# Gate and up tiles of two feed-forward blocks as seven block products, on one Trainium2 core

## The chip, the core and the metric

One core of one Trainium2 chip runs the whole program. The metric is device time in microseconds. Five engines work side by side, each with an instruction queue of its own: TensorE (PE in the rows, its weight loads PEld), VectorE (DVE), ScalarE (ACT), GpSimd (POOL) and SyncE (SP), which issues the loads. Instructions wait for one another through semaphores. TensorE writes PSUM, eight banks of 128 partitions x 512 float32.

## The reference, cut to what matters

One layer of a streaming encoder works on 288 tokens: 256 of a prompt and 32 new frames of a running stream.

```
h = x + 1/2 * swiglu(rmsnorm(x, g_ffn1), w1_gate, w1_up, w1_down)
h = h + token_mix(rmsnorm(h, g_mix), ...)          # pooling branch and attention
h = h + 1/2 * swiglu(rmsnorm(h, g_ffn2), w2_gate, w2_up, w2_down)
y = rmsnorm(h, g_final)

swiglu(x, wg, wu, wd) = (silu(x @ wg) * (x @ wu)) @ wd
```

The model width is 2048 (16 tiles of 128), the hidden width of each feed-forward block 5632 (44 tiles of 128). All data are float32. The change lies in the two swiglu blocks.

## The kernel before, in words

Tokens lie along the free dimension: an activation is 16 tiles of [128, 288], and a weight block of 128x128 is the stationary operand. To keep float32 accuracy at the speed of the shorter float32r type, each operand is split into a hi part (a cast) and a lo part (the difference), and each product is three matmuls: hi x hi, hi x lo, lo x hi (`mac`, lines 156 to 160).

The program is a list of steps (`step`, line 82). A step that needs weights names a source; `run` (line 91) issues its load on SyncE five steps ahead, splits it two steps ahead (`split_into`, lines 191 to 193: the cast on ScalarE, the subtraction raw - hi on VectorE; raw and hi lie both in SBUF), and then emits the step's matmuls. Work that follows a step, such as taking a result out of PSUM, is put off by `later`. So the order in each engine's queue is the order in which `run` emits.

`ffn` (line 279) takes the 44 hidden tiles in four chunks of 11. For each hidden tile it makes gate and up (16 blocks each, two loads of 128x1024), scales by the row norm, applies SiLU and the product, and splits the result (`post_g`, `post_u`). Then come 16 down tiles, each over the 11 hidden tiles of the chunk, added into h by `post_d` on VectorE. In the first block the first two hidden tiles are done apart, while the tokens arrive (`first_tiles`).

Between the two blocks lies the token mixer. Only one piece of it matters below: `post_z` (line 392) builds window sums on GpSimd (line 405), beside VectorE's subtractions of weights (line 193), and `scores4` and `attend4` (lines 707 to 734) use four column tiles of 32 for the new frames of four heads.

Of the kernel before, what the change touches and what calls it, by code (L numbers as in the profile page):

```python
# [33 lines left out]
CHUNKS = ((0, 11), (11, 22), (22, 33), (33, 44))  # L34
TB = T // 3

T_BUFS = 78
RAW_BUFS = 5
SPLIT_BUFS = 4
LOAD_AHEAD = 5  # L40
# [6 lines left out]
def kernel(ctx: ExitStack, tc: tile.TileContext, i, o):  # L47
# [10 lines left out]
    b4 = ctx.enter_context(tc.tile_pool(name="b4", bufs=4))  # L58
    psa = ctx.enter_context(tc.tile_pool(name="psa", bufs=8, space=bass.MemoryType.PSUM))
# [27 lines left out]

    def later(lag, fn):
        due.append((now[0] + lag, fn))

    def run():
        weighted = [k for k, s in enumerate(steps) if s[0] is not None]
        raws, splits = {}, {}
        at = [0, 0, 0]

        def load_to(n):
            while at[0] < min(n, len(weighted)):
                k = weighted[at[0]]
                src, m, _, extra, _, _ = steps[k]
# [3 lines left out]
                sp.dma_start(out=raw[:, :m], in_=src)  # L103
                raws[k] = raw
                at[0] += 1

        def split_some(n, count):

            while at[1] < min(n, len(weighted)) and count:
                k = weighted[at[1]]  # L110
                m, extra = steps[k][1], steps[k][4]
                if k not in splits:
# [13 lines left out]
                if c.stop == m:  # L126
                    raws.pop(k)
                    at[1] += 1

        done = 0  # L130
        load_to(LOAD_AHEAD)
        start()
        for k, (src, n, fn, _, _, late) in enumerate(steps):
            now[0] = k
            load_to(done + 1 + LOAD_AHEAD)
            split_some(done + 1, 99)
            if late is None:
                split_some(done + 1 + SPLIT_AHEAD, 99)
# [77 lines left out]
    def norm_part(st, x, first, last):  # L216
        if first:
            st["sum"] = acc()
        for j in range(3):
            pe.matmul(st["sum"][:TB, j : j + 1], x[:, j * TB : (j + 1) * TB], ones[:, 0:1],  # L220
                      start=first and j == 0, stop=last and j == 2)

    def norm_sum(st, width):
# [4 lines left out]
        v = sm.tile([TB, 3], F32, tag="v", name="v")  # L228
        dve.tensor_scalar(v, ps[:TB, 0:3], 1.0 / width, EPS, op0=ALU.mult, op1=ALU.add)
        r = sm.tile([TB, 3], F32, tag="r3", name="r3")  # L230
        pool.tensor_tensor(out=r, in0=v, in1=mhalf, op=ALU.pow)
        st["r3"] = r

    def norm_spread(st, scale=1.0, copy=True):
        ps = acc()
        for j in range(3):
            pe.matmul(ps[:, j * TB : (j + 1) * TB], st["r3"][:, j : j + 1].to_broadcast([TB, P]), ident[:TB, :TB],
                      start=True, stop=True)
# [12 lines left out]
    mhalf = cst.tile([TB, 3], F32, name="mhalf")  # L251
    prompt_p = [[cst.tile([P, (b + 1) * P], F32, name=f"p{q}{b}") for b in range(2)] for q in range(2)]
    gains = {n: cst.tile([P, w], F32, name=n) for n, w in
             (("g1", KD), ("gm", KD), ("g2", KD), ("gf", KD), ("gq", KL), ("gkv", KL), ("psc", 8))}
    cosT = cst.tile([P, T], F32, name="cosT")
    sinT = cst.tile([P, T], F32, name="sinT")
    inv16 = cst.tile([P, 4, 16], F32, name="inv16")
    hist = cst.tile([P, 8, HIST], F32, name="hist")

    krz = [cst.tile([P, S], F32, name=f"krz{j}") for j in range(2)]  # L260
    krh = cst.tile([P, SEQ], F32R, name="krh")
    krl = [cst.tile([P, SEQ], F32R, name=f"krl{j}") for j in range(2)]
    ckvh = cst.tile([P, KL, S], F32R, name="ckvh")
    ckvl = cst.tile([P, KL, S], F32R, name="ckvl")
    ckvn = cst.tile([P, KL, P], F32R, name="ckvn")
    pfar = cst.tile([P, P], F32, name="pfar")
    pnew = cst.tile([P, P], F32, name="pnew")
    osam = cst.tile([P, P], F32, name="osam")
# [9 lines left out]

    def ffn(wg, wu, wd, xs, st, last, together=None):
        extra = [lambda: norm_sum(st, D), lambda: norm_spread(st)]  # L280
        for c, (f0, f1) in enumerate(CHUNKS):
            mid = ({}, {})
            sv = {}

            def post_g(ps, m, sv=sv):
                z = col("z")
                dve.tensor_tensor(out=z, in0=ps[:, :T], in1=st["r"], op=ALU.mult)  # L287
                sv[m] = col("s")
                act.activation(sv[m], z, AF.Silu)  # L289

            def post_u(ps, m, sv=sv, mid=mid):
                u = col("u")
                dve.tensor_tensor(out=u, in0=ps[:, :T], in1=st["r"], op=ALU.mult)  # L293
                g = col("g")
                dve.tensor_tensor(out=g, in0=u, in1=sv.pop(m), op=ALU.mult)
                mid[0][m], mid[1][m] = split_dve(g, "m")

            if together is not None and c == 0:
                f0 += 2
                together(post_g, post_u)  # L300
            for m in range(f0, f1):
                for w, post in ((wg, post_g), (wu, post_u)):
# [3 lines left out]
                    if first:  # L306
                        step(extra.pop(0))
            f0 = CHUNKS[c][0]
            for m in range(KD):
# [7 lines left out]
                def post_d(ps, m=m, fin=(c == len(CHUNKS) - 1)):  # L317
                    dve.scalar_tensor_tensor(out=h[m], in0=ps[:, :T], scalar=0.5, in1=h[m], op0=ALU.mult, op1=ALU.add)
                    if fin:
                        last(m)  # L320
# [657 lines left out]
```

## Time and profile before

| | us |
|---|---|
| median of 3 runs (2435.15 to 2435.42) | 2435.3 |
| profiled execution | 2435.43 |
| its span | 2433.4 |
| TensorE busy | 2420.4 |
| VectorE busy | 1380.1 |
| ScalarE busy | 994.2 |
| GpSimd busy | 54.8 |

The span is the time from the first to the last instruction of the profiled execution; its own time is a little longer. Matmuls are pipelined, and their durations overlap: what one costs in a stream is the distance from one start or end to the next. A row of the timeline gives start, duration, engine, line, operation, output and inputs, form and count; two or more instructions of one line that follow each other closely are merged into one row with a count and their joint duration. A busy VectorE or GpSimd instruction can be one that stands and waits: its duration tells both.

### The profile page before, as it was taken

To read this page: it belongs to the slowest core of one execution; us is meant where nothing else is said; L and a number is where in the kernel's file an instruction comes from. 1 tells how busy PE (TensorE), PEld (TensorE's weight loads), DVE (VectorE), ACT (ScalarE), POOL (GpSimd) and SP (SyncE) were. 2 spreads that over 40 slices of the span, in tenths; PEclk is the share of its full clock that TensorE was granted. 3 is DMA by queue.
4 is the path that set the end of the run, shared out by engine and by line. 5 is a ranking of instruction groups with operands and counts; after the bars stand their busy time and mean duration, and the time that the engine had idled before them with its cause. 6 is when DMAs were issued, how large, how long until landed. Compare 5 with 4: busy or idle time off the path is not lost.

```text
span 2433.4 us, 43918 instructions
## 1 busy us (share of the span) xinstructions
PE 2420.4 (99%) x18312; PEld 2414.3 (99%) x18312; DVE 1380.1 (57%) x2057; ACT 994.2 (41%) x1475; POOL 54.8 (2%) x94
## 2 busy tenths in 40 slices
PE   9999999999999999999999999999999999999998
PEld 9999999999999999999999999999999999999998
DVE  7555555555555776544467666555555555555555
ACT  6333333333333535433377634433333333333344
POOL 0000000000000150000000000000000000000000
PEclk9999999999999999999999999999999999999999
DMA  7555446545554755544423355544554464455444
GB/s 241 175 147 186 165 146 178 176 161 149 188 166 146 215 166 167 184 168 165 156 101 101 118 199 175 172 159 167 150 185 166 148 187 164 159 155 186 166 145 128
DMA packets 129014, 399.71 MB, mean 164 GB/s; under 512 B 16160, under 2 KB 21536, under 8 KB 128816
## 3 DMA queue, kind: packets, MB, share of 16 engines
q1 hardware_dynamic: 126592, 392.73, 50.8%
q8 instruction: 143, 2.34, 0.4%
q0 software_dynamic: 1504, 3.15, 0.4%
q10 hardware_dynamic: 720, 1.04, 0.1%
q14 instruction: 55, 0.45, 0.1%
HBM read 391.35 MB, written 5.51 MB: 163 GB/s over the span
## 4 chain that ended last, share of the span: by engine, by line
PE 64%; issue 34%; DVE 1%; ACT 0%; DMA 0%; SPq 0%; POOLq 0%; POOL 0%; DVEq 0%; ACTq 0%
PE acc L159 20%; PE acc L158 20%; PE acc L160 20%; PE acc L633 0%; PE acc L634 0%; PE acc L635 0%; PE acc L696 0%; DVE wlo L193 0%; DVE y L874 0%; DMA raw<-in_ws 0%; PE acc L629 0%; PE acc L628 0%; PE acc L671 0%; PE acc L670 0%; PE acc L697 0%
## 5 line engine op out<-in xcount | busy, mean ns | idle before, releaser
L193 DVE TENSOR_TENSOR wlo<-raw,whi 128x1024 fp32r<-128x1024 f32 (+2 forms) x856 | 916.4, 1075 | 663.4 <-ACT whi L192 660.0
L192 ACT CAST whi<-raw 128x1024 fp32r<-128x1024 f32 (+2 forms) x858 | 788.8, 924 | 916.0 <-PE acc L159 751.3
L158 PE MATMUL acc<-xh,whi 128*128 128x288 f32 x3584 | 1057.3, 295 | 0.8 <-ACT whi L192 0.8
L160 PE MATMUL acc<-xh,wlo 128*128 128x288 f32 x3584 | 1056.6, 295 | 1.1 <-DVE wlo L193 1.1
L159 PE MATMUL acc<-xl,whi 128*128 128x288 f32 x3584 | 1057.4, 295 | 0.0
L160 PEld LDWEIGHTS acc<-xh,wlo 128*128 128x128 f32 x3584 | 673.5, 188 | 1.8 <-DVE wlo L193 1.8
L158 PEld LDWEIGHTS acc<-xh,whi 128*128 128x128 f32 x3584 | 673.5, 188 | 1.4 <-ACT whi L192 1.4
L159 PEld LDWEIGHTS acc<-xl,whi 128*128 128x128 f32 x3584 | 674.3, 188 | 0.0
L159 PE MATMUL acc<-ml,whi 128*128 128x288 f32 x1408 | 415.1, 295 | 0.0
L160 PE MATMUL acc<-mh,wlo 128*128 128x288 f32 x1408 | 414.7, 295 | 0.0
L158 PE MATMUL acc<-mh,whi 128*128 128x288 f32 x1408 | 414.2, 294 | 0.0
L159 PEld LDWEIGHTS acc<-ml,whi 128*128 128x128 f32 x1408 | 264.6, 188 | 0.0
L160 PEld LDWEIGHTS acc<-mh,wlo 128*128 128x128 f32 x1408 | 264.5, 188 | 0.0
L158 PEld LDWEIGHTS acc<-mh,whi 128*128 128x128 f32 x1408 | 264.5, 188 | 0.0
L289 ACT ACTIVATE s<-z 128x288 f32<-128x288 f32 x88 | 39.0, 445 | 232.5 <-DVE z L287 232.4
L287 DVE TENSOR_TENSOR z<-acc,r 128x288 f32<-128x288 f32 x88 | 40.1, 457 | 87.9 <-PE acc L160 83.8
L293 DVE TENSOR_TENSOR u<-acc,r 128x288 f32<-128x288 f32 x88 | 40.2, 457 | 83.4 <-PE acc L160 83.4
L158 PE MATMUL acc<-oh,whi 128*128 128x288 f32 x256 | 76.1, 297 | 0.0
L159 PE MATMUL acc<-ol,whi 128*128 128x288 f32 x256 | 75.6, 295 | 0.0
L160 PE MATMUL acc<-oh,wlo 128*128 128x288 f32 x256 | 75.5, 295 | 0.0
L158 PE MATMUL acc<-mgh,whi 128*128 128x288 f32 x256 | 75.4, 295 | 0.0
L160 PE MATMUL acc<-mgh,wlo 128*128 128x288 f32 x256 | 75.3, 294 | 0.0
(207 smaller groups left out, 1821.2 us busy)
## 6 DMA issues: line engine op xcount, KB each, us to landing
raw<-in_wg SPq DMA_DIRECT2D x172, 512.0 KB, 3.3
raw<-in_wu SPq DMA_DIRECT2D x172, 512.0 KB, 3.3
raw<-in_wd SPq DMA_DIRECT2D x128, 384.0 KB, 3.3
raw<-in_wd SPq DMA_DIRECT2D x128, 320.0 KB, 3.0
raw<-in_wga SPq DMA_DIRECT2D x32, 512.0 KB, 3.3
raw<-in_wgb SPq DMA_DIRECT2D x32, 512.0 KB, 3.3
raw<-in_wo SPq DMA_DIRECT2D x32, 512.0 KB, 3.3
raw<-in_wout SPq DMA_DIRECT2D x32, 512.0 KB, 3.4
```

Source lines behind the costliest of these rows:

```text
L158: pe.matmul(out, hi[:, c], xh, start=first, stop=False)
L159: pe.matmul(out, hi[:, c], xl, start=False, stop=False)
L160: pe.matmul(out, lo[:, c], xh, start=False, stop=last)
L192: act.copy(hi, src)
L193: dve.tensor_tensor(out=lo, in0=src, in1=f(hi), op=ALU.subtract)
L287: dve.tensor_tensor(out=z, in0=ps[:, :T], in1=st["r"], op=ALU.mult)
L289: act.activation(sv[m], z, AF.Silu)
L293: dve.tensor_tensor(out=u, in0=ps[:, :T], in1=st["r"], op=ALU.mult)
```

## The change

Hidden tiles 4 to 43 are taken in 10 groups of four (`GROUP`), in both blocks; tiles 0 to 3 stay as they were. For a group and two neighbouring tiles of the model width (k even, k odd) the prompt's work is a product of two 2x2 block matrices: the tokens (first and second 128, by k even and odd) times the weights (k even and odd, by gate and up). It is made with seven products in place of eight. Such a set is a unit; a group has eight, and all eight add up in seven PSUM banks.

- The tokens (128x128, hi and lo) are the stationary operand now and the weights (128x512: four hidden tiles) the moving one. Sums of the tokens are made once for each block (`sums`: GpSimd, with copies on ScalarE, then a split) and kept.
- The weights' combinations t1, t2, t4, t3 are four subtractions on GpSimd for each unit (`prepare`). Each of the seven operands is then split by ScalarE and VectorE (`make`, line 236 being the subtraction).
- The 32 new frames don't take part: `frames` multiplies them with the unsplit weights in float32, in four column tiles of 32, for two units at a time.
- At the end of a group `ends` combines the seven banks, with norm, SiLU and product, tokens along the partitions. `turned` transposes the result back on TensorE, during the down tiles of the group before, and splits it.
- The down product runs for each group of four hidden tiles, one load of 128x512 for each of the 16 output tiles, so that h is added to 11 times and not 4.
- Loads of gate and up take rows of 1 KB (256 columns of four hidden tiles). Up to six loads are held, and up to eight operands of 128x512 are split ahead (`room`).
- The norm is split at 128, 128 and 32 tokens, not three times 96. Constants of the mixer share buffers with the kept sums and are set up between the blocks (`take`, `fresh`).

```diff
-CHUNKS = ((0, 11), (11, 22), (22, 33), (33, 44))
+GROUP = 4
+GROUPS = KF // GROUP
+W = GROUP * P
+PARTS = ((0, P), (P, P), (SEQ, DEC))
+ORDER = ("b11", "b21", "b22", "t1", "t2", "t4", "t3")
-T_BUFS = 78
-RAW_BUFS = 5
+T_BUFS = 76
+RAW_BUFS = 6
...
+        def room(done):
+            n, used = done, 0
+            while n < len(weighted) and used + cost[n] <= 2 * SPLIT_BUFS - 1:
+                used += cost[n]
+                n += 1
+            return n
...
-            split_some(done + 1, 99)
+            load_some()
+            if src is not None:
+                split_some(done + 1, 99)
             if late is None:
-                split_some(done + 1 + SPLIT_AHEAD, 99)
+                split_some(room(done), 99)
...
+        def sums(i):
...
+            for k in (k1, k2):
+                xg = col("xg")
+                act.activation(xg, h[k], AF.Copy, scale=gain[:, k : k + 1])
+                act.copy(new[k // 8][:, k % 8, :], xg[:, SEQ:])
+                a.append((xg[:, :P], xg[:, P:SEQ]))
+            (a11, a21), (a12, a22) = a
...
+            pool.tensor_tensor(out=s1, in0=a21, in1=a22, op=ALU.add)
+            pool.tensor_tensor(out=s2, in0=s1, in1=a11, op=ALU.subtract)
+            pool.tensor_tensor(out=s3, in0=a11, in1=a21, op=ALU.subtract)
+            pool.tensor_tensor(out=s4, in0=a12, in1=s2, op=ALU.subtract)
...
+            def prepare():
+                b11, b12, b21, b22 = (four(u[w], k) for w, k in (("g", 0), ("u", 0), ("g", 1), ("u", 1)))
+                u.update(b11=b11, b21=b21, b22=b22)
+                t = {}
+                for n, (pl, tag) in (("t1", (b3, "vs")), ("t2", (b2, "v")), ("t4", (b2, "v")), ("t3", (b3, "vs"))):
+                    t[n] = pl.tile([P, W], F32, tag=tag, name=n)
+                    u[n] = t[n][:, :].rearrange("p (m c) -> p m c", m=GROUP)
+                    x, y = {"t1": lambda: (b12, b11), "t2": lambda: (b22, u["t1"]), "t4": lambda: (b21, u["t2"]),
+                            "t3": lambda: (b22, b12)}[n]()
+                    pool.tensor_tensor(out=u[n], in0=x, in1=y, op=ALU.subtract)
+            def make(name):
...
+                w = wsp.tile([P, 2 * W], F32R, tag=tag, name=tag)
+                hi, lo = w[:, :W], w[:, W:]
+                split_into(*(x.rearrange("p (m c) -> p m c", m=GROUP) for x in (hi, lo)), u.pop(name))
...
+            def body(name, hi, lo):
...
+                pe.matmul(bank[name], sh, hi, start=not i, stop=False)
+                pe.matmul(bank[name], sl, hi, start=False, stop=False)
+                pe.matmul(bank[name], sh, lo, start=False, stop=end)
+                if end:
+                    ends(name, bank)
+            def frames():
...
+                for k in range(2):
+                    x = new[(2 * i + k) // 8][:, (2 * i + k) % 8, :]
+                    for q in range(4):
+                        raw = u["g" if q > 1 else "u"][:, :].rearrange("p (m k c) -> p k m c", m=GROUP, k=2)
+                        pe.matmul(bank["new"][32 * q : 32 * q + 32, : 2 * P], x, raw[:, k, 2 * (q % 2) : 2 * (q % 2) + 2, :],
+                                  start=not i and not k, stop=i == KD // 2 - 1 and k == 1)
...
+        def ends(name, bank):
+            r = st["r3"]
+            if name == "b11":
+                bank["a"] = tmp(b2, "v")
+                act.copy(bank["a"], bank.pop("b11"))
+            elif name == "b21":
+                g = bank["g1"] = tmp(b3, "vs")
+                dve.tensor_tensor(out=g, in0=bank.pop("b21"), in1=bank["a"], op=ALU.add)
+                act.activation(g, g, AF.Silu, scale=r[:, 0:1])
...
+        for c in range(1, GROUPS):
+            bank = {"c": c}
+            units = [unit((wg, wu), i, bank) for i in range(KD // 2)]
+            for i in range(KD // 2):
+                if i % 2 == 0:
+                    step(lambda a=units[i][0], b=units[i + 1][0]: (a(), b()))
+                for fn, make, srcs in units[i][1]:
+                    operand(fn, make, srcs)
+            down(c - 1, bank)
+        down(GROUPS - 1)
```

How this moves instructions, at three places.

VectorE's queue in the gate and up stage, before: the rows of one hidden tile (wlo is the lo half of a weight load, z and u are the scaled gate and up, mh and ml the split result).

```order
L193 TENSOR_TENSOR wlo<-raw,whi 128x1024 x2
L287 TENSOR_TENSOR z<-acc,r 128x288
L193 TENSOR_TENSOR wlo<-raw,whi 128x1024 x2
L293 TENSOR_TENSOR u<-acc,r 128x288
L295 TENSOR_TENSOR g<-u,s 128x288
L197 CAST mh<-g 128x288
L198 TENSOR_TENSOR ml<-g,mh 128x288
```

And the same queue now: one unit, and the first row of the next (whi and wlo are two rings of buffers here, each holding the hi and the lo half of one operand; raw is a load, t1 to t3 come from GpSimd).

```order
L236 TENSOR_TENSOR whi_2201<-raw_2062,whi_2201 128x512
L236 TENSOR_TENSOR wlo_2207<-raw_2062,wlo_2207 128x512
L236 TENSOR_TENSOR whi_2213<-raw_2064,whi_2213 128x512
L236 TENSOR_TENSOR wlo_2223<-t1_2193,wlo_2223 128x512
L236 TENSOR_TENSOR whi_2229<-t2_2195,whi_2229 128x512
L236 TENSOR_TENSOR wlo_2235<-t4_2197,wlo_2235 128x512
L236 TENSOR_TENSOR whi_2241<-t3_2199,whi_2241 128x512
L236 TENSOR_TENSOR wlo_2255<-raw_2092,wlo_2255 128x512
```

Per pair of model tiles and four hidden tiles there were two instructions of 1024 columns' worth of this kind (four of 512); now there are seven of 512, and nothing else stands between them until the group ends.

GpSimd's queue from the start of the program to the mixer, before (r is the norm, hspill a store).

```order
L337 MEMSET krz_103 64x416
L338 MEMSET krl_106 64x256
L337 MEMSET krz_104 64x416
L338 MEMSET krl_107 64x256
L339 MEMSET pnew 64x128
L231 TENSOR_TENSOR r_679<-v,mhalf 96x3
L376 DMA hspill<-h 128x288 x16
L231 TENSOR_TENSOR r_9480<-v,mhalf 96x3
```

And in the gate and up stage now: two units.

```order
L421 TENSOR_TENSOR t1_1309<-raw_1180,raw_1178 128x512
L421 TENSOR_TENSOR t2_1311<-raw_1180,t1_1309 128x512
L421 TENSOR_TENSOR t4_1313<-raw_1178,t2_1311 128x512
L421 TENSOR_TENSOR t3_1315<-raw_1180 128x512
L421 TENSOR_TENSOR t1_1363<-raw_1210,raw_1208 128x512
L421 TENSOR_TENSOR t2_1365<-raw_1210,t1_1363 128x512
L421 TENSOR_TENSOR t4_1367<-raw_1208,t2_1365 128x512
L421 TENSOR_TENSOR t3_1369<-raw_1210 128x512
```

GpSimd had nothing to do in this stage; it now has four instructions for each seven of VectorE's, each reading two SBUF operands.

VectorE's queue where gate and up end and down begins, before.

```order
L193 TENSOR_TENSOR wlo_1845<-raw_1747,whi_1844 128x768
L293 TENSOR_TENSOR u_1867<-acc_1783,r_746 128x288
L295 TENSOR_TENSOR g_1869<-u_1867,s_1810 128x288
L197 CAST mh_1871<-g_1869 128x288
L198 TENSOR_TENSOR ml_1872<-g_1869,mh_1871 128x288
L193 TENSOR_TENSOR wlo_1878<-raw_1777,whi_1877 128x640
L193 TENSOR_TENSOR wlo_1899<-raw_1812,whi_1898 128x768
L318 SCALAR_TENSOR_TENSOR h_117<-acc_1848,h_117 128x288
```

And now: after the split of the last unit's last operand come the first output operation (line 485) and the split for the first down tile, and then, from the second to the fourth down tile's split, these rows (out is an output of the group, acc a PSUM bank).

```order
L236 TENSOR_TENSOR wlo_2392<-raw_2218,whi_2391 128x512
L489 TENSOR_TENSOR out_2371<-acc_1975,out_2371 128x512
L490 TENSOR_TENSOR out_2398<-acc_1968,out_2371 128x512
L491 TENSOR_TENSOR out_2398<-acc_1957,out_2398 128x512
L492 SCALAR_TENSOR_TENSOR out_2398<-out_2398,r3_660,out_2376 128x512
L236 TENSOR_TENSOR wlo_2409<-raw_2310,whi_2408 128x512
L496 TENSOR_TENSOR out_2371<-acc_1989,out_2371 128x512
L497 TENSOR_TENSOR out_2415<-acc_1968,out_2371 128x512
L498 TENSOR_TENSOR out_2371<-acc_1982,out_2371 128x512
L502 SCALAR_TENSOR_TENSOR mnew_1912<-acc_1911,r3_660,gnew_2420 64x256
L506 SCALAR_TENSOR_TENSOR out_2415<-out_2415,r3_660,out_2371 128x512
L236 TENSOR_TENSOR wlo_2440<-raw_2312,whi_2439 128x512
```

Ten output operations, that of the new frames among them, now stand among the splits for the first four down tiles. On ScalarE the group's SiLU stands ahead of the first down tile's cast, and the second SiLU and the new frames' ahead of the fourth's.

## Rows read from the trace of the kernel before

**Rows 1.** The page: busy times, and shares of the chain that ended last.

```profile
PE 2420.4 (99%) x18312; PEld 2414.3 (99%) x18312; DVE 1380.1 (57%) x2057; ACT 994.2 (41%) x1475; POOL 54.8 (2%) x94
...
PE 64%; issue 34%; DVE 1%; ACT 0%; DMA 0%; SPq 0%; POOLq 0%; POOL 0%; DVEq 0%; ACTq 0%
```

**Rows 2.** Stages: us; PE, PEld, DVE, ACT, POOL busy (count); PEclk, DMA share, GB/s.

```profile
10.00:20.00 10.00, 10.00 (x78) 10.00 (x77) 10.00 (x22) 10.00 (x24) 0.00 (x0) 1.00 0.96 312
...
2000.00:2100.00 100.00, 100.00 (x758) 100.00 (x757) 53.87 (x70) 36.23 (x40) 0.00 (x0) 1.00 0.50 167
```

**Rows 3.** Groups by line and form: busy us, mean ns | idle before, releasers.

```profile
L158 PE MATMUL acc<-xh,whi 128*128 128x288 f32 x3584 | 1057.3, 295 | 0.8 <-ACT whi L192 0.8
L160 PE MATMUL acc<-xh,wlo 128*128 128x288 f32 x3584 | 1056.6, 295 | 1.1 <-DVE wlo L193 1.1
...
L193 DVE TENSOR_TENSOR wlo<-raw,whi 128x1024 fp32r<-128x1024 f32 x516 | 633.1, 1229 | 458.1 <-ACT whi L192 457.5 <-DMA raw<-in_wq 0.5
...
L193 DVE TENSOR_TENSOR wlo<-raw,whi 128x512 fp32r<-128x512 f32 x84 | 55.0, 684 | 7.8 <-ACT whi L192 7.6
L192 ACT CAST whi<-raw 128x512 fp32r<-128x512 f32 x86 | 50.2, 618 | 8.8 <-PE acc L159 5.3 <-DMA raw<-in_ws 1.7 <-issue 1.2
```

**Rows 4.** Timeline of TensorE in the mixer: start us, us, engine, line, operation.

```profile
1242.20 0.28 PE L634 MATMUL acc<-whi,ckvl 128*128 128x256 f32 x1
1242.32 0.28 PE L635 MATMUL acc<-wlo,ckvh 128*128 128x256 f32 x1
1242.44 0.27 PE L685 MATMUL acc<-ident,p 128*128 128x128 f32 x1
1242.55 0.27 PE L686 MATMUL acc<-ident,p 128*128 128x128 f32 x1
...
1247.78 0.35 PE L158 MATMUL acc<-ckvh,whi 128*128 128x416 f32 x1
1247.97 0.35 PE L159 MATMUL acc<-ckvl,whi 128*128 128x416 f32 x1
...
1262.27 0.28 PE L677 MATMUL acc<-krl,qrs 128*128 128x256 f32 x1
1262.48 0.48 PE L711 MATMUL acc<-kn,qn 128*32 128x160 f32 x8
1262.78 0.45 PE L713 MATMUL acc<-krz,qr 128*32 128x160 f32 x8
1263.16 0.46 PE L158 MATMUL acc<-ckvh,whi 128*128 128x416 f32 x1
```

**Rows 5.** Timeline of VectorE at the start, where it has no gaps.

```profile
11.31 0.68 DVE L193 TENSOR_TENSOR wlo<-raw,whi 128x512 fp32r<-128x512 f32 x1
11.91 0.45 DVE L209 TENSOR_TENSOR sq<-sq 128x288 f32<-128x288 f32 x1
```

**Rows 6.** VectorE and GpSimd in the pooling branch; line 405 with min/median/max ns.

```profile
875.87 0.71 POOL L405 TENSOR_TENSOR win<-z 128x317 f32<-128x317 f32 x1 [2.15 <-DVE z L399]
876.15 1.51 DVE L193 TENSOR_TENSOR wlo<-raw,whi 128x1024 fp32r<-128x1024 f32 x1 [0.43 <-ACT whi L192]
876.66 1.57 POOL L405 TENSOR_TENSOR win<-win 128x315 f32<-128x315 f32 x1
877.59 0.68 DVE L412 TENSOR_TENSOR pd<-win,inv 128x16 f32<-128x16 f32 x1
...
878.30 0.18 DVE L413 TENSOR_TENSOR pd<-pd,z 128x16 f32<-128x16 f32 x1
...
879.65 1.22 DVE L193 TENSOR_TENSOR wlo<-raw,whi 128x1024 fp32r<-128x1024 f32 x1
...
L405 POOL TENSOR_TENSOR win<-win x12: 734/820/1573, 871.7 to 904.5; 128x315 f32<-128x315 f32 x6, 128x311 f32<-128x311 f32 x4, 128x303 f32<-128x303 f32 x2
...
L405 POOL TENSOR_TENSOR win<-z x8: 709/711/1632, 863.6 to 901.3; 128x317 f32<-128x317 f32 x8
```

**Rows 7.** GpSimd's product for the rotary tables, which nothing held up.

```profile
992.11 0.80 POOL L456 TENSOR_TENSOR sr<-sinT,r 128x288 f32<-128x288 f32 x1
```

More of the change, by code (lines that the diff above doesn't have):

```diff
@@ L218, in norm_part @@
             st["sum"] = acc()
-        for j in range(3):
-            pe.matmul(st["sum"][:TB, j : j + 1], x[:, j * TB : (j + 1) * TB], ones[:, 0:1],
-                      start=first and j == 0, stop=last and j == 2)
+        for j in (0, 2, 1):
+            t0, n = PARTS[j]
+            pe.matmul(st["sum"][:n, j : j + 1], x[:, t0 : t0 + n], ones[:, 0:1], start=first and j == 0, stop=last and j == 1)
     def norm_sum(st, width):
@@ L268 @@
-    osam = cst.tile([P, P], F32, name="osam")
-    h = {}
-    x1, x2, x3 = ({}, {}), ({}, {}), ({}, {})
-    n1, n2, n3, n4, nkv, nq = {}, {}, {}, {}, {}, {}
-    def enter(k, src, gain, xs, st):
-        xs[0][k], xs[1][k] = split_act(src, gain[:, k : k + 1], "x")
-        square_into(st, src)
[L279 to L302, printed above, removed]
-                    first = bool(extra)
-                    linear(halves(w, m), lambda: xs, lambda ps, m=m, post=post: post(ps, m),
-                           lag=1 if not first else 4 if w is wg else 2)
[L306 to L309, printed above, removed]
-                blocks = []
-                k = f0
-                while k < f1:
-                    n = min(6, f1 - k)
-                    blocks.append((wd[m, :, k * P : (k + n) * P], k, n))
-                    k += n
[L317 to L320, printed above, removed]
-                linear(blocks, lambda mid=mid: mid, post_d)
@@ L325, in start, with take @@
-    def start():
-        dve.memset(ones, 1.0)
-        act.copy(pfar, ones)
-        keep_warm(WARM)
-        make_identity(nc, ident)
-        dve.memset(mhalf, -0.5)
+    quarter = cst.tile([P, P], F32, name="quarter")
+    krl = [None, cst.tile([P, SEQ], F32R, name="krl1")]
+    prompt_p = cosT = sinT = inv16 = hist = krz = krh = ckvh = ckvl = ckvn = pnew = osam = pfar = None
+    def take(dt, *shapes):
+        t = kp.tile([P, 2 * W], dt, tag="kp", name="kept")
+        views, at = [], 0
+        for a, *b in shapes:
+            n = a * (b[0] if b else 1)
+            v = t[:, at : at + n]
+            views.append(v.rearrange("p (a b) -> p a b", a=a) if b else v)
+            at += n
+        return views
@@ L341, in load_gains, with start @@
+    def start():
+        dve.memset(ones, 1.0)
+        act.copy(quarter, ones)
+        keep_warm(WARM)
+        make_identity(nc, ident)
+        dve.memset(mhalf, -0.5)
+        for q in range(4):
+            pool.tensor_copy(quarter[:, 32 * q : 32 * q + 32], ident[:, 0:32])
     def load_gains():
```

253 lines of the change are left out of this document (209 added, 44 removed).

## The prediction

> **What bounds the kernel now.** I read the busy times of the page first: TensorE is busy 99% of the span, VectorE 57%, ScalarE 41% and GpSimd 2% [rows 1]. The chain that ended last is TensorE's work or its own issue for 98%, so time is spent where TensorE has instructions, and nearly nothing elsewhere [rows 1]. The stage table then gives its pace in the two feed-forward blocks: 758 matmuls in 100 us, 0.132 us for one of 288 columns, at the full granted clock (1.00, the 2.4 GHz level) [rows 2]. The groups by line show what has to keep up: ScalarE's cast and VectorE's subtraction of every weight tile, 0.618 and 0.684 us for 128x512 [rows 3]. Both wait for TensorE or for each other and hold nobody up: the matmuls waited 0.8 and 1.1 us for them in the whole run [rows 3].
>
> A group of 4 of the 44 feed-forward tiles costs today 384 gate and up matmuls and 192 down matmuls, 576 x 0.132 = 76.0 us. The change touches 10 such groups in each of two blocks, 20 in all.
>
> **The change on TensorE.** Each group now has 8 units of 7 products, each product 3 matmuls of 512 columns. The trace has none of that width. The starts of 256, 288 and 416 columns lie 0.12, 0.132 and 0.19 us apart [rows 2, 4], that is 12 to 16 ns above columns/2.4 GHz; for 512 I take 213 + 15 = 0.228 us. A unit is 21 x 0.228 = 4.79 us.
>
> The new frames add, for each pair of units, 16 float32 matmuls of 32 stationary columns and 256 moving ones, in four column tiles. Float32 takes two instructions each: eight of 160 columns, over four column tiles, end 0.27 us after the eight before them (1262.96 to 1263.23) [rows 4]; one after the other at 2 cycles a column they would take 8 x 0.133 = 1.07 us. So the four tiles do run side by side. For 256 columns this is 0.27 x 256/160 = 0.43 us, four times in a pair 1.72 us. Entry costs 0.14 us (the first eight end 0.41 us after what stood before) and leaving 0.20 us (the next matmul of 416 columns ends 0.39 us on and not 0.19) [rows 4]. A pair of units is 2 x 4.79 + 2.06 = 11.6 us, a group's gate and up 46.6 us against 50.7 us now. Ten transposes return the tokens to columns: three in the trace start 0.11 us apart [rows 4], 1.1 us. Down keeps its 192 matmuls, 25.3 us. TensorE alone would take 73.0 us for a group and gain 3.0 us.
>
> **The change on the engines that feed it.** A unit needs 7 casts on ScalarE, 7 x 0.618 = 4.3 us, and 7 subtractions on VectorE, 7 x 0.684 = 4.8 us [rows 3]; back to back a 128x512 subtraction delays the next instruction by 0.60 us (11.31 to 11.91) [rows 5], so 4.2 us. Either fits beside 5.8 us of TensorE. What is new is GpSimd: 4 subtractions of 128x512 in a unit, on an engine that is idle in this stage today.
>
> The rows of the pooling branch decide what those cost. At 876.15 VectorE's weight subtraction, which reads two SBUF operands as the new ones do, takes 1.51 us and not 1.22 as at 879.65: it ends 1.08 us after GpSimd's sum of 875.87 has ended. GpSimd's next sum, at 876.66, takes 1.57 us where such a sum takes 0.71 to 0.74 alone; it ends 0.57 us after VectorE's. The 16-column product behind it needs 0.68 us, and the same shape at 878.30 0.18 [rows 6]. The two engines take turns: while one reads two SBUF operands, the other waits, and only 0.14 to 0.16 us of the waiting instruction's own time is saved. After VectorE's instruction the waiting GpSimd one goes first.
>
> So a turn in the new stage is one VectorE subtraction, 0.684 - 0.14 = 0.545 us, and one GpSimd subtraction. For that: the remainder of 0.57 us for 315 columns gives 0.93 for 512; the products with the rotary tables, 0.80 us for 288 columns that nothing held up [rows 7], give (0.80 - 0.16) x 512/288 = 1.14. I take 1.0, nearer to the sums, and 1.545 us for a turn. In a unit, 4 turns and 3 lone subtractions come to 4 x 1.545 + 3 x 0.60 = 8.0 us against TensorE's 5.8: the pair VectorE and GpSimd becomes what the stage waits for.
>
> What of a group's gate and up stands under it: the operands run at most 8 ahead (8 buffers of one operand each), so the first unit is split beside the last down tiles. When TensorE enters the stage it spends 2.06 us on frames and 0.68 us on a product before the next buffer is free, and the cast takes 0.62 us: 3.4 us in which GpSimd has its next five subtractions done. Then 48 VectorE subtractions remain and 23 GpSimd ones of the six later units: 23 x 1.545 + 25 x 0.60 = 50.5 us, and one matmul, 0.3 us. Sum 54.2 us, 7.6 us over TensorE's own.
>
> **The end of a group.** The order of VectorE's queue puts the group's ten output operations, the new frames' among them, among the splits of the first four down tiles. From the last operand's subtraction on: the gate's sum (0.62), the SiLU on ScalarE (0.62) and only behind it, in ScalarE's queue, the first down tile's cast (0.62); first and second split done at 2.6 and 3.2 us; four output operations (2.5) and the third split 6.4; three more, two activations on ScalarE, the fourth tile's cast, two products and its split, about 11. TensorE could have been through three tiles (each 12 x 0.132 = 1.58 us) by 5 us and stands before the third and fourth until then: 5.5 us lost in a group, 4.0 to 6.5 with each row's shortest and longest. (Output operations of 512 columns at 0.62 us, the casts' duration in [rows 3] and VectorE's pace in [rows 5]; the new frames' narrow ones at 0.4 us, a little under the 288-column one there.) Later down tiles give VectorE 0.60 + 0.45 us of work [rows 5] against 1.58 us, in which it makes up its lead; the eleven additions into h where there were four are hidden there.
>
> **The rest.** Column sums of the tokens, once in each block, put 8 x 2.1 us on ScalarE (two scaled copies at 0.54, two narrow ones at 0.2 and a cast at 0.62, an estimate) beside four gate and up tiles of 25 us where it already has 16 x 0.62 = 9.9 of casts [rows 3]: up to 2 us a block, 4 us in all. Loads in rows of 1 KB: the nearest rows are the mixed 1.1 and 2 KB rows at the start, 312 GB/s from 10 to 20 us [rows 2]; a unit needs 1 MB in 6.8 us, 154 GB/s, so I cost them at nothing; if the rate fell below that, the loads would be the new pace.
>
> **Sum.** A group: 54.2 + 25.3 + 1.1 + 5.5 = 86.1 us against 76.0; 20 x 10.1 = 202 us, and 4. The profiled execution took 2435.4 us, of which the span is 2433.4; the median of the runs is 2435.3. Forecast 2641, said as 2640 us. Bounds of its own: turns of 1.475 us (0.93 on GpSimd) and 4.0 us at the group's end give 83.0 us a group and 2579; the rotary rate makes 1.685 a turn, 57.5 us, and with 6.5 us at the end 90.4 and 2727.
>
> **Rivals.** (a) The turns don't bind: GpSimd's work slips into VectorE's gaps. Then a group is 46.6 + 26.4 and, since splits run seven operands ahead, about 2.0 us at its end: 75.0, 20 us less over 20 groups, 2419 with the sums. For it: VectorE and GpSimd would have gaps if work were light. Against it: even without any overhead 23 x 0.93 + 48 x 0.545 = 47.6 us of exclusive time stand in a stage of 46.6. It decides if GpSimd's turn falls under about 0.7 us for 512 columns, below every row.
>
> (b) Full turns: nothing of the waiting instruction's fixed time is saved. With 0.71 x 512/317 = 1.15 us: 23 x (0.684 + 1.15) + 25 x 0.684 + 3.7 = 63.0, with 26.4 and 6.5 a group of 95.9 us, 2837. For it: queues here are fuller than in the pooling branch; against it, both directions in [rows 6] save 0.14 us or more. The Trainium skill's page "SBUF — State Buffer" (section "Who interferes with whom") says that the loser blocks until the other's whole instruction is over; by that rule the sum would be this rival's, and the trace agrees that they exclude each other but not to the last 0.14 us.
>
> (c) The column tiles run one after the other when all four read the moving weights through wide strides: 16 x 2 x 0.213 + 0.34 = 7.2 us a pair, 67 us of TensorE in a stage, 95.5 a group with 2 us at its end, 2829. Against it stand the four heads of [rows 4], with four different moving operands.
>
> **Chances.** Forecast 0.65, (a) 0.14, (b) 0.12, (c) 0.06; 0.03 for a time within 0.2% (about 5 us, the least that a measurement tells from no change), between (a) and the forecast. Faster by more than 0.2% is (a), 0.14; within 0.03; slower 0.83. The likeliest case alone spans 2575 to 2730; the range reaches up to (b) and down to where the turns bind but the group's end is hidden (54.2 + 26.4 = 80.6 us, 2531), a little below: 2500 to 2840.
>
> **What would show it.** Right: GpSimd near half busy in the gate and up stages, its 128x512 subtractions with means well over 1.15 us; VectorE's at 1 us and more and waiting for nobody; TensorE's idle time put down to VectorE's lo halves; stages of about 54 us and a standstill of several us at the third and fourth down tile; eight 32-column matmuls of a step ending 0.43 us apart. Wrong: VectorE's 128x512 still at 0.68 us beside a busy GpSimd, or TensorE without idle time in the stage.

## The result: 2960 us instead of 2435 us, and the profile after

The changed kernel takes 2960.0 us (2958.4 to 2963.2, 4 runs) against 2435.2 us: 1.216 times as long, interval 1.214 to 1.218. The forecast was 2640 us with a range of 2500 to 2840. The sign and the mechanism came out; the size did not: 525 us are lost, not 205.

The page of the changed kernel, busy times, chain and the new groups (busy us, mean ns of one | idle before):

```profile
PE 2566.6 (87%) x16756; PEld 2138.7 (72%) x16756; DVE 2429.2 (82%) x3161; ACT 1400.9 (47%) x2611; POOL 1139.0 (39%) x828
DVE 45%; PE 40%; issue 11%; ACT 3%; POOL 1%; DMA 0%; DVEq 0%; ACTq 0%; SPq 0%
L421 POOL TENSOR_TENSOR t<-raw 128x512 f32<-128x512 f32 x320 | 536.0, 1690 | 601.6 <-DMA raw<-in_wu 501.0
L421 POOL TENSOR_TENSOR t<-raw,t 128x512 f32<-128x512 f32 x320 | 512.0, 1600 | 266.9 <-DVE wlo L236 127.4
L236 DVE TENSOR_TENSOR wlo<-raw,wlo 128x512 fp32r<-128x512 f32 x240 | 408.2, 1701 | 16.6 <-ACT wlo L235 16.4
L236 DVE TENSOR_TENSOR whi<-t,whi 128x512 fp32r<-128x512 f32 x320 | 314.3, 982 | 0.0
L236 DVE TENSOR_TENSOR wlo<-t,wlo 128x512 fp32r<-128x512 f32 x320 | 304.5, 952 | 0.0
```

Against [rows 1], TensorE falls from 99% to 87% and the chain passes to VectorE. VectorE's subtraction of 128x512, 0.684 us in [rows 3], has means of 0.95 to 1.70 us in the units, and hardly waits for anybody there. The stage table says the same of 100 us, after [rows 2]; its columns are those:

```profile
300.00:400.00 100.00, 83.11 (x502) 62.67 (x503) 93.70 (x109) 46.49 (x86) 52.14 (x33) 0.98 0.42 127
```

In one unit of a gate and up stage the turns can be seen one by one; VectorE first, then GpSimd (start us, us):

```profile
301.88 1.78 DVE L236 TENSOR_TENSOR wlo<-t,wlo 128x512 fp32r<-128x512 f32 x1
303.58 1.77 DVE L236 TENSOR_TENSOR whi<-raw,whi 128x512 fp32r<-128x512 f32 x1
305.27 1.77 DVE L236 TENSOR_TENSOR wlo<-raw,wlo 128x512 fp32r<-128x512 f32 x1
306.96 1.77 DVE L236 TENSOR_TENSOR whi<-raw,whi 128x512 fp32r<-128x512 f32 x1
308.66 0.68 DVE L236 TENSOR_TENSOR wlo<-t,wlo 128x512 fp32r<-128x512 f32 x1
309.26 0.68 DVE L236 TENSOR_TENSOR whi<-t,whi 128x512 fp32r<-128x512 f32 x1
309.86 0.68 DVE L236 TENSOR_TENSOR wlo<-t,wlo 128x512 fp32r<-128x512 f32 x1
301.50 3.30 POOL L421 TENSOR_TENSOR t<-raw,t 128x512 f32<-128x512 f32 x2 [1.90 <-DVE wlo L236]
304.76 3.43 POOL L421 TENSOR_TENSOR t<-raw 128x512 f32<-128x512 f32 x2
```

Four subtractions start 1.70 us apart, each with one of GpSimd's beside it, and three 0.60 us apart, in which GpSimd stands still: 4 x 1.70 + 3 x 0.60 = 8.6 us for a unit, and TensorE needs under 6.

I measure a group by the same copy (line 482) in two groups:

```profile
244.27 0.59 ACT L482 COPY out<-acc 128x512 f32<-128x512 f32 x1 [1.80 <-DVE whi L236]
343.29 0.59 ACT L482 COPY out<-acc 128x512 f32<-128x512 f32 x1 [1.79 <-DVE whi L236]
```

That is 99.0 us here and 99.2 in the mean of 18, where [rows 2] gave 76.0 and the forecast was 86.1. So 20 x 23.2 = 464 of the 525 us lie in the groups, if the two first ones cost as much as the 18 measured; the remaining 61 lie at the beginning and the end of the blocks.

### The profile page after: what moved, and what is told of

Same layout as the page of the kernel before. It is cut to its first block, busy times and chain, and to the rows that moved or that the text cites. A ratio compares the mean times of both kernels' runs of the same rounds, so it can differ in the third digit from the quotient of the medians.

```text
span 2957.1 us, 45597 instructions
## 1 busy us (share of the span) xinstructions
PE 2566.6 (87%) x16756; PEld 2138.7 (72%) x16756; DVE 2429.2 (82%) x3161; ACT 1400.9 (47%) x2611; POOL 1139.0 (39%) x828
## 4 chain that ended last, share of the span: by engine, by line
DVE 45%; PE 40%; issue 11%; ACT 3%; POOL 1%; DMA 0%; DVEq 0%; ACTq 0%; SPq 0%
DVE wlo L236 20%; DVE whi L236 19%; PE acc L203 12%; PE acc L201 12%; PE acc L202 12%; ACT whi L235 1%; DVE hre L539 1%; DVE h L539 1%; PE acc L530 1%; DVE out L497 0%; DVE out L490 0%; DVE out L491 0%; DVE out L498 0%; DVE out L485 0%; ACT wlo L235 0%
## 5 line engine op out<-in xcount | busy, mean ns | idle before, releaser
L421 POOL TENSOR_TENSOR t<-raw 128x512 f32<-128x512 f32 x320 | 536.0, 1690 | 601.6 <-DMA raw<-in_wu 501.0
L235 ACT CAST whi<-raw 128x512 fp32r<-128x512 f32 (+1 forms) x874 | 609.7, 713 | 317.1 <-PE acc L202 259.3
L236 DVE TENSOR_TENSOR wlo<-raw,whi 128x512 fp32r<-128x512 f32 (+1 forms) x632 | 539.8, 863 | 199.9 <-ACT whi L235 189.5
L421 POOL TENSOR_TENSOR t<-raw,t 128x512 f32<-128x512 f32 x320 | 512.0, 1600 | 266.9 <-DVE wlo L236 127.4
L236 DVE TENSOR_TENSOR wlo<-raw,wlo 128x512 fp32r<-128x512 f32 x240 | 408.2, 1701 | 16.6 <-ACT wlo L235 16.4
L236 DVE TENSOR_TENSOR whi<-raw,whi 128x512 fp32r<-128x512 f32 x242 | 388.8, 1607 | 0.0
L201 PE MATMUL acc<-xh,whi 128*128 128x288 f32 x1024 | 305.1, 298 | 7.0 <-ACT whi L235 5.4
L203 PE MATMUL acc<-xh,wlo 128*128 128x288 f32 x1024 | 304.1, 297 | 5.3 <-DVE wlo L236 5.2
L202 PE MATMUL acc<-xl,whi 128*128 128x288 f32 x1024 | 303.3, 296 | 0.2 <-DVE xl L231 0.2
L201 PEld LDWEIGHTS acc<-xh,whi 128*128 128x128 f32 x1024 | 194.2, 190 | 8.3 <-ACT whi L235 6.4
```

The lines of the kernel that those rows point to most:

```text
L201: pe.matmul(out, hi[:, c], xh, start=first, stop=False)
L202: pe.matmul(out, hi[:, c], xl, start=False, stop=False)
L203: pe.matmul(out, lo[:, c], xh, start=False, stop=last)
L235: act.copy(hi, src)
L236: dve.tensor_tensor(out=lo, in0=src, in1=f(hi), op=ALU.subtract)
L421: pool.tensor_tensor(out=u[n], in0=x, in1=y, op=ALU.subtract)
```

## The experiments

| kernel | us | one group, us |
|---|---|---|
| before | 2435.2 | 76.0 |
| after | 2960.0 | 99.2 |
| no frames | 2970.4 | 99.7 |
| no differences in the first unit | 2894.8 | 96.2 |
| differences on VectorE | 2715.3 | 87.0 |
| VectorE reads one operand | 2676.3 (one run) | 85.0 |
| GpSimd copies | 2559.3 (one run) | 79.3 |
| GpSimd fills | 2553.9 (one run) | 79.3 |
| no differences | 2549.8 | 79.4 |
| the same, sums once | 2529.7 | 79.3 |
| the same, last stage later | 2525.9 | 79.3 |
| the same, gates later | 2478.0 | 75.8 |
| the last four together | 2437.4 | 75.8 |
| whole computation, best order found | 2620.2 | 83.2 |

### Is it GpSimd's work, or the arrangement?

Differences on VectorE:
```diff
-                    pool.tensor_tensor(out=u[n], in0=x, in1=y, op=ALU.subtract)
+                    dve.tensor_tensor(out=u[n], in0=x, in1=y, op=ALU.subtract)
```


> The four subtractions of a unit run on VectorE instead of GpSimd; nothing else changes. Turns theory (VectorE and GpSimd exclude each other, and a turn of 1.70 us sets the pace of the stage): a unit is then 7 splits and 4 subtractions back to back on VectorE, 11 x 0.60 = 6.6 us instead of 8.59, still over TensorE's 5.8; 8 units lose 16 us of 99.2 us, and 20 groups 320 us: 2640 us (2600 to 2720), with VectorE's 128x512 subtractions back at 0.68 us. Rival, the arrangement itself costs (frames, the end of a group, the half clock there, loads of 1 KB rows): VectorE gets more work and TensorE's waits stay, 2900 us or more.

Measured 2715.3 us (ratio to before 1.115, 1.113 to 1.117), at the upper end of what the turns gave. VectorE does 57% more subtractions in a unit, and the kernel is 245 us faster.

No differences:
```diff
-                t = {}
...
-                    pool.tensor_tensor(out=u[n], in0=x, in1=y, op=ALU.subtract)
+                u.update(t1=b12, t2=b22, t4=b21, t3=b12)
```


> The four differences of a unit are left out: the products take the raw blocks in their place (another output), and GpSimd has nothing to do in the gate and up stages. Turns theory: a unit falls from 8.59 us to TensorE's 5.8, gate and up from 65.2 to 48 us, the end of a group and the half clock there stay: 99.2 - 17 = 82 us a group, 2960 - 20 x 17 = 2620 us (2560 to 2660). Rival, the arrangement itself costs: TensorE's waits stay and the run is over 2800 us. Rival (a) of the prediction in another dress, that all but the turns is cheaper than before: under 2435 us.

Measured 2549.8 us (1.047, 1.045 to 1.048), a little under the range. So GpSimd's 640 subtractions cost 410 of the 525 us, and 115 us are another matter.

No frames:
```diff
-                for k in range(2):
+                for k in range(0 if i else 1):
```


> The changed kernel with its turns, but the float32 column tiles of the new frames are run only once in a group instead of four times per two units (their sums are left out, so the output is another). They take 2.06 us of TensorE for two units, 7.7 us of a group's 99.2. Turns theory: TensorE waits in every unit anyway, so its saved time becomes waiting: 2960 us, at the least 2900 where the beginning of a stage gains something. Rival, TensorE's own longer work makes the stage slow: 20 x 7.7 = 155 us less, 2805 us.

Measured 2970.4 us (1.220, 1.218 to 1.221): some 145 us of TensorE's work are gone (an estimate: 15 of 16 parts of the 1.93 us that the frames of two units take below, four times in 20 groups), and nothing is gained. That shows that TensorE's work does not set the pace of the gate and up stage. (Why it is 10 us more was not followed; the mean granted clock of this run is 0.969 and not 0.979.)

### What makes a turn

GpSimd copies in one run, and fills in another:
```diff
-                    pool.tensor_tensor(out=u[n], in0=x, in1=y, op=ALU.subtract)
+                    pool.tensor_copy(u[n], x if n in ("t1", "t3") else y)
```
```diff
-                    pool.tensor_tensor(out=u[n], in0=x, in1=y, op=ALU.subtract)
+                    pool.memset(u[n], 0.0)
```


> GpSimd copies one operand of each of its subtractions instead of subtracting (the second operand is left out, so the output is another), with the same tiles and the same order. Turns theory as the prediction had it (only two SBUF operands on both sides exclude each other): VectorE's subtraction returns to 0.68 us and the run falls to that of the kernel without GpSimd's work, about 2600 us. Wider turns theory (VectorE's two-operand instruction excludes any GpSimd instruction that reads SBUF): VectorE's subtractions beside them stay well over 0.8 us and each copy has a mean over its length alone by some 0.5 us; with a copy of 0.5 to 0.8 us a turn is 1.0 to 1.3 us and the run 2650 to 2800 us.

> GpSimd fills the four tiles of a unit with zeros and reads nothing (the differences are left out, so the output is another). Turns theory, narrow or wide: an instruction that reads no SBUF takes no turn, VectorE's 128x512 subtractions are back at 0.68 us and the run is at that of the kernel without GpSimd's work, about 2600 us. Rival, GpSimd's writes exclude VectorE too: VectorE's subtractions beside a fill take over 0.8 us.

The run with copies took 2559.3 us, which was the narrow theory's number. Its trace has the wide theory's mechanism: VectorE in the gate and up stage, and one GpSimd row:

```profile
338.70 1.02 DVE L236 TENSOR_TENSOR whi<-t,whi 128x512 fp32r<-128x512 f32 x1
339.64 1.09 DVE L236 TENSOR_TENSOR wlo<-raw,wlo 128x512 fp32r<-128x512 f32 x1
340.66 1.09 DVE L236 TENSOR_TENSOR whi<-raw,whi 128x512 fp32r<-128x512 f32 x1
341.68 1.09 DVE L236 TENSOR_TENSOR wlo<-raw,wlo 128x512 fp32r<-128x512 f32 x1
342.69 0.68 DVE L236 TENSOR_TENSOR whi<-t,whi 128x512 fp32r<-128x512 f32 x1
340.14 2.09 POOL L421 COPY t<-raw 128x512 f32<-128x512 f32 x2
```

A copy, which reads one operand, takes turns too, 1.02 us each. Then a unit of VectorE is 4 x 1.02 + 3 x 0.60 = 5.9 us, just what TensorE needs, and the turns are hidden. My time for the wide theory was too high because I took every turn as a loss, without the room that VectorE has in a unit. The run with fills took 2553.9 us, and there are no turns in it, by these groups:

```profile
L421 POOL MEMSET t<- 128x512 f32 x640 | 319.8, 525 | 1173.3 <-DVE wlo L236 666.0 <-DVE whi L236 285.2 <-DVE out L506 219.5
L236 DVE TENSOR_TENSOR wlo<-raw,wlo 128x512 fp32r<-128x512 f32 x240 | 166.2, 692 | 158.7 <-ACT wlo L235 158.4
```

VectorE is back at 0.69 us: against VectorE's two-operand subtraction it is GpSimd's reading that excludes, not its writing.

VectorE reads one operand:
```diff
-                split_into(*(x.rearrange("p (m c) -> p m c", m=GROUP) for x in (hi, lo)), u.pop(name))
...
+                act.copy(h3, src)
+                dve.tensor_scalar(l3, src, 1.0, None, op0=ALU.mult)
```


> GpSimd subtracts as in the changed kernel, and VectorE's splits of the units read one SBUF operand (a product with 1) instead of two (the low halves are left out, so the output is another). What is told apart is which side's operands make the turns. If VectorE must read two operands to exclude GpSimd's subtraction: VectorE's instructions take their length alone, GpSimd's subtractions 1.28 us, and since 4 x 1.28 = 5.1 us fits a unit of 5.8 the run is near that without differences, 2550 to 2600 us. If any VectorE instruction excludes it: GpSimd's subtractions stay at 1.5 us or more, units over 6.5 us, 2650 to 2960 us.

Measured 2676.3 us, in the range of the second theory, but neither is quite right. With one operand VectorE's instruction is nearly twice as fast, and at that pace it takes turns as well:

```profile
347.35 0.41 DVE L434 TENSOR_SCALAR wlo<-t 128x512 fp32r<-128x512 f32 x1
347.69 0.41 DVE L434 TENSOR_SCALAR whi<-t 128x512 fp32r<-128x512 f32 x1
349.80 1.51 DVE L434 TENSOR_SCALAR wlo<-raw 128x512 fp32r<-128x512 f32 x1
351.23 1.50 DVE L434 TENSOR_SCALAR whi<-raw 128x512 fp32r<-128x512 f32 x1
350.99 2.90 POOL L421 TENSOR_TENSOR t<-raw 128x512 f32<-128x512 f32 x2
```

Alone these instructions start 0.34 us apart and not 0.60, in turns 1.43. The edit changed the number of operands and the pace at once; one operand from SBUF at the slower pace was not tried. That not every VectorE instruction excludes GpSimd's is shown by the addition into h, which reads one operand from PSUM and one from SBUF: it takes 0.45 us beside a GpSimd subtraction (376.87 below).

One formula fits the three kernels. GpSimd's shortest durations, of instructions that nothing held up and called "alone" here, are these, in the changed kernel and in that with copies (min/median/max ns):

```profile
L421 POOL TENSOR_TENSOR t<-raw x320: 1263/1732/1843, 57.4 to 2862.5; 128x512 f32<-128x512 f32 x160
L421 POOL TENSOR_TENSOR t<-raw,t x320: 1291/1612/2152, 58.7 to 2861.0; 128x512 f32<-128x512 f32 x160
```
```profile
L421 POOL COPY t<-raw x320: 602/1069/1603, 58.0 to 2462.3; 128x512 f32<-128x512 f32 x160
```

A turn is GpSimd's time alone plus VectorE's spacing, less about 0.18 us: 1.28 + 0.60 - 0.18 = 1.70; 1.28 + 0.34 - 0.18 = 1.44 (1.43 measured); 0.60 + 0.60 - 0.18 = 1.02. The Trainium skill's page "SBUF — State Buffer" (section "Who interferes with whom") says that GpSimd shares a port pair with VectorE's second one, that a VectorE instruction with two SBUF inputs contends with a GpSimd instruction that reads SBUF, that one in a two-port mode contends with GpSimd, and that the loser blocks for the whole instruction. The runs bear out who excludes whom, in each case tried (of the product with 1 they show the faster pace, not the mode); "whole" is measured as all but 0.18 us.

### Was the first unit done ahead?

```diff
+                if not i:
+                    u.update(t1=b12, t2=b22, t4=b21, t3=b12)
+                    return
```


> The changed kernel, but the first of the eight units of every group takes raw blocks in place of its four differences (another output); the other seven units are untouched. The prediction counted the first unit's splits and five GpSimd subtractions as done ahead, beside the last down tiles: then leaving out four of them changes nothing, 2950 to 2965 us. Against it: VectorE is late already in the down stage, the first unit's turns stand in one row with all others and each costs its 1.10 us beyond a lone split: 4 x 1.10 = 4.4 us less in a group of 99.2 us, 2960 - 88 = 2870 us (2860 to 2910).

Measured 2894.8 us (1.189, 1.187 to 1.190): 65 us less; a group is 3.0 us shorter, of the 4.4 that four turns cost beyond lone splits. They were not done ahead. The trace of the changed kernel shows why; GpSimd's first subtraction for the stage, VectorE at the passage from down tiles to units, and TensorE's entry:

```profile
373.40 1.29 POOL L421 TENSOR_TENSOR t<-raw 128x512 f32<-128x512 f32 x1 [32.54 <-DMA raw<-in_wu]
375.38 1.56 DVE L236 TENSOR_TENSOR wlo<-raw,wlo 128x512 fp32r<-128x512 f32 x1
376.87 0.45 DVE L539 SCALAR_TENSOR_TENSOR h<-acc,h 128x288 f32<-128x288 f32 x1
377.23 1.43 DVE L236 TENSOR_TENSOR whi<-raw,whi 128x512 fp32r<-128x512 f32 x1
378.58 1.78 DVE L236 TENSOR_TENSOR wlo<-raw,wlo 128x512 fp32r<-128x512 f32 x1
384.60 0.68 DVE L236 TENSOR_TENSOR wlo<-t,wlo 128x512 fp32r<-128x512 f32 x1
385.57 1.40 DVE L236 TENSOR_TENSOR whi<-raw,whi 128x512 fp32r<-128x512 f32 x1
379.40 1.93 PE L464 MATMUL acc<-raw,xs 128*32 128x256 f32 x32
```

The first unit's own splits (375.38 on) are in turns with GpSimd; the seventh, at 384.60, starts 5.2 us after TensorE has entered the stage, and only then the second unit's begin. GpSimd could not start earlier either: its first subtraction was released by the landing of its load, 6.0 us before TensorE's entry (4.2 to 6.0 us in the 18 groups that follow another). The last row also answers for the column tiles: 32 instructions in 1.93 us, where the forecast was 1.72 + 0.34 = 2.06 for two units.

### The 115 us that are not turns

Without differences, a group is 79.4 us. TensorE's standstill at its end, in that kernel:

```profile
289.82 0.40 PE L201 MATMUL acc<-mh,whi 128*128 128x288 f32 x1 [2.35 <-ACT whi L235]
290.95 0.61 PE L203 MATMUL acc<-mh,wlo 128*128 128x288 f32 x1 [0.60 <-DVE wlo L236]
```

In the changed kernel the same gap (2.36 and 0.60 us) is followed by this stretch, in which the granted clock is 0.56, for most of it the 1.2 GHz level, and matmuls of 288 columns are 0.24 us apart and not 0.13:

```profile
356.40:360.30 3.90, 3.90 (x19) 3.90 (x19) 3.58 (x8) 0.77 (x2) 0.00 (x0) 0.56 0.62 191
360.30:373.50 13.20, 13.20 (x104) 13.20 (x103) 10.18 (x23) 6.47 (x16) 0.10 (x1) 1.00 0.64 187
```

Gates later:
```diff
-                act.activation(a, a, AF.Silu, scale=r[:, 1:2])
...
-                later(1, finish)
+                def gates():
+                    act.activation(a, a, AF.Silu, scale=r[:, 1:2])
...
+                later(2, gates)
+                later(3, finish)
```


> No differences (as in the run that left them out, 2549.8 us and 79.3 us a group), and the two SiLU activations at a group's end with the product behind them stand two down tiles later in the queues of ScalarE and VectorE, so that the fourth down tile's cast no longer waits behind them. Theory: the standstill of 2.35 + 0.60 us before the fourth down tile goes, and with it the stretch at half clock behind it (1.6 us): about 3.5 of 79.3 us a group, 70 us in all, 2480 us (2460 to 2505). Rival: the wait passes to the next down tile and the end of a group costs the same, 2540 to 2555 us.

Measured 2478.0 us (1.017, 1.015 to 1.019). What is left of the gap is 0.80 and 0.26 us, and no stretch at half clock follows:

```profile
205.47 0.40 PE L203 MATMUL acc<-mh,wlo 128*128 128x288 f32 x1 [0.80 <-DVE wlo L236]
207.60 0.40 PE L203 MATMUL acc<-mh,wlo 128*128 128x288 f32 x1 [0.26 <-DVE wlo L236]
205.50:209.50 4.00, 3.74 (x26) 3.49 (x27) 3.39 (x8) 3.14 (x7) 0.31 (x1) 1.00 0.42 117
```

In ScalarE's queue the fourth tile's cast had stood behind two activations, and in VectorE's queue its subtraction behind two products. The edit moves both, which was not tried apart; together with the stretch at half clock that was worth 72 us.

Sums once (for the first pair alone, and there as copies on VectorE, which all eight pairs then use):
```diff
+            if i:
+                return
...
-            pool.tensor_tensor(out=s1, in0=a21, in1=a22, op=ALU.add)
...
+                dve.tensor_copy(t[:, j * P : j * P + P], x)
...
-            return kept[i][:, c : c + P], kept[i][:, c + W : c + W + P]
+            return kept[0][:, c : c + P], kept[0][:, c + W : c + W + P]
```


> No differences, and the column sums of the tokens are made for the first pair only and used for all eight (so the output is another); the scaled copies on ScalarE stay. The run without differences is 114.5 us over the kernel before, of which 20 groups of 79.3 instead of 76.0 us make 66. Theory: the sums' chain from ScalarE over GpSimd to VectorE at the head of each block makes the other 48 us: 2505 us (2500 to 2520). Rival: the first groups are late for another reason, such as the change from tile loads to block loads or the first units' splits: 2535 to 2550 us.

Measured 2529.7 us (1.039, 1.037 to 1.040), between the two: the sums with their splits are 20 us, not 48. Its trace showed where the rest is. The last down stage of the first block, VectorE and ScalarE:

```profile
878.51 0.44 DVE L532 SCALAR_TENSOR_TENSOR h<-acc,h 128x288 f32<-128x288 f32 x1
879.55 0.52 DVE L231 SCALAR_TENSOR_TENSOR xl<-h,gm,xh 128x288 fp32r<-128x288 f32 x1 [0.60 <-ACT xh L230]
880.39 0.69 DVE L236 TENSOR_TENSOR wlo<-raw,whi 128x512 fp32r<-128x512 f32 x1
881.00 0.45 DVE L532 SCALAR_TENSOR_TENSOR h<-acc,h 128x288 f32<-128x288 f32 x1
878.98 0.54 ACT L230 ACTIVATE xh<-h,gm 128x288 fp32r<-128x288 f32 x1 [1.30 <-DVE h L532]
879.42 0.43 ACT L246 ACTIVATE sq<-h 128x288 f32<-128x288 f32 x1
879.75 0.60 ACT L235 CAST whi<-raw 128x512 fp32r<-128x512 f32 x1
```

The addition releases ScalarE's copy, the square and the next cast stand behind it, VectorE's subtraction waits for the cast, and the next addition stands behind that: a ring of 2.50 us for a tile whose matmuls take 1.58. Before, a column of down tiles was 11 tiles deep and the additions 4.4 us apart, so the ring was hidden.

Last stage later:
```diff
-                    last(m)
+                    last(m) if m == KD - 1 else later(1, lambda: last(m))
```


> No differences (2549.8 us so), and in the last down stage of each block what follows the addition into h (the next block's operands and squares) stands one down tile later in the queues of ScalarE and VectorE. In the trace these last tiles end 2.50 us apart, and not 1.58: the addition, ScalarE's scaled copy and square, the next cast behind them and VectorE's subtraction add up to 0.45 + 0.54 + 0.43 + 0.45 + 0.62 = 2.5 us in a ring through both queues. Theory: the ring opens, the tiles end at most 1.9 us apart, and the two stages give back most of 2 x 16 x 0.92 = 29 us: 2522 us (2515 to 2532). Rival: these tiles are slow for the work itself or for the loads: 2545 to 2553 us.

Measured 2525.9 us (1.037, 1.036 to 1.039): 24 us. The additions come 1.77 us apart, and VectorE has no gap between them:

```profile
876.04 0.45 DVE L533 SCALAR_TENSOR_TENSOR h<-acc,h 128x288 f32<-128x288 f32 x1
877.81 0.44 DVE L533 SCALAR_TENSOR_TENSOR h<-acc,h 128x288 f32<-128x288 f32 x1
```

### Together

The floor takes the last three edits without differences. The best order found keeps the whole computation, with the differences on VectorE, the gates later and the last stage later.

> The floor of this arrangement: no differences, sums for the first pair only (another output), the SiLU activations two down tiles later and the work behind the last down tiles one tile later. Theory: the four costs are separate and add up, 2549.8 - 72 - 20 - 28 = 2430 us (2420 to 2445), within half a per cent of the kernel before: TensorE's own work has become hardly shorter. Rival: the costs cover one another and the run stays over 2455 us; or TensorE's forecast time of 73.0 us a group is reached, 2385 us or less.

> What the runs have given so far, with the whole computation kept: the four subtractions of a unit on VectorE (2715.3 us), the two SiLU activations at a group's end two down tiles later, and the work behind the last down tiles one tile later. Theory: 3.5 us of each of 20 groups go if VectorE has room there, less if its 11 subtractions of a unit are already late there, and 25 us at the two last down stages: 2640 us (2610 to 2665), still over the kernel before by the 6.6 us that a unit needs of VectorE against TensorE's 5.8 and by the sums. Rival: with VectorE as the bound nothing moves, 2700 us or more.

The floor took 2437.4 us, 1.0009 of before (1.0000 to 1.0018): the costs add up, and with all of them gone and the differences left out, the arrangement only comes back to where it started. The best order took 2620.2 us (1.076, 1.074 to 1.077), 340 us less than the changed kernel and still slower than before.

## Why the prediction was wrong

**Right: the turns.** VectorE and GpSimd exclude each other, the pair sets the pace of the stage, lone splits are 0.60 us, the rate of the loads doesn't bind (the floor moves the same weights in 75.8 us a group), and the frames' column tiles run side by side. Rival (a) fell with that, and rival (c) with the frames' 1.93 us. Rival (b) came nearer in time (95.9 us a group, measured 99.2), but by luck: its turn of 1.83 us is too long, since both sides do save a little, and it gave the same credit at the start of a stage as the forecast.

**Wrong: one GpSimd subtraction in a turn, 1.0 us.** Measured, 1.70 - 0.545 = 1.155. The two rows it was taken from gave 0.93 and 1.14, and I chose a value nearer to the sums. The rotary products [rows 7], scaled to 512 columns, were right. The sums of [rows 6] take less for a column, alone too (0.71 us for 317 columns, against 1.28 for the 512 of a subtraction); why is not shown. 23 turns x 0.155 = 3.6 us a group, 71 us in all.

**Wrong: the credit at the start of a stage.** "3.4 us in which GpSimd has its next five subtractions done", and the first unit split beside the last down tiles. Five subtractions of 1.28 us alone are 6.4 us, and they aren't alone: while VectorE still splits the first unit, they take turns with it. With the first unit's four they are nine, 11.5 us alone, and from GpSimd's start to 3.4 us after TensorE's entry there were 9.4 us at most. Counting all of them, 32 x 1.70 + 24 x 0.60 = 68.8 us, and a stage took 65.2 (99.2 less 34.0 from the last gate and up matmul to the frames). The forecast was 54.2; after the 3.6 above, 7.4 us a group or 148 us in all are this step. The run without the first unit's differences shows 60 us of them directly (20 x 3.0); the rest is by this count.

**Nearly right: the end of a group.** The forecast lost 5.5 us; the stretch from the last gate and up matmul to the frames was 34.0 us, not 31.9. TensorE's gaps in it were 0.91, 0.20, 0.59, 2.36 and 0.60 us in the group shown, 4.7 in all and a little under the forecast. The half clock behind the gap was not foreseen and makes some 1.5 us, most of the difference (an estimate: 14 matmuls 0.24 us apart and not 0.13). TensorE did stand before the fourth down tile, as forecast; moving the gates gave back 3.6 us a group, in the kernel without differences.

**Too high: TensorE's gain.** 73.0 us a group were forecast. With everything out of the way a group takes 75.8, of which TensorE is busy 74.7: matmuls of 512 columns end 0.233 us apart and not 0.228 (0.8 us a group), and the down stage with its transposes takes 28.5 us with its small gaps and not 26.4. The 60 us that should have paid for something were 4.

**Missed: beginning and end of a block.** Forecast 4 us, measured 61. Shown, in the kernel without differences, are 20 us for the sums and 24 us for the ring in the last down stage. Of the ring the prediction had nothing: it cost down as 192 matmuls and did not ask what stands behind a tile when the column is 4 deep. Of the other 17 us some 14 go with the differences: without them the beginnings and ends cost 115 - 20 x 3.4 = 47 us. In a block's first group the sums and the differences share GpSimd's queue; what of the 14 us that makes was not tried apart.

Together: 464 us in the groups were forecast as 202. Of the missing 262 the turn's size and the credit make 219, and the half clock and the small gaps at the end of a group 42; another 57 us were missed at the beginnings and ends of the blocks.

## What to carry to other kernels

Before work goes to GpSimd, add the time of its instruction alone to that of each VectorE instruction that reads two SBUF operands, or, like the product with 1, one at the faster pace, beside it. In these runs such instructions and GpSimd's that read SBUF went one after the other, but for 0.18 us of each turn. Give no credit for work "done ahead" on an engine that shares with the one that is late. When a loop is cut into shorter pieces, look at what stands behind each piece's end in every in-order queue: a cast behind an activation, or an addition behind a cast, was hidden by the long piece.

## What the runs showed of the hardware

- A GpSimd copy that reads one SBUF operand (0.60 us alone) took turns with VectorE's two-operand subtraction; a fill (0.53 us) did not.
- VectorE's fp32 product with a constant, 512 columns, started 0.34 us apart, where the subtraction does 0.60, and took turns all the same. Its addition of a PSUM tile into h took 0.45 us beside GpSimd's subtraction (376.87 above), as alone.
- GpSimd's two-operand subtraction of 128x512 took 1.26 to 1.29 us alone, its copy 0.60.
- After gaps of 2.36 and 0.60 us in TensorE's work the granted clock was 0.56 for 3.9 us; after gaps of 0.80 and 0.26 us it stayed at 1.00.
